# Decay broadcasts on SP's queue, and the first block's decays behind the latest eviction, in a hybrid SSD and linear-attention layer

## The chip, the cores and the metric

The kernel runs on one core of a Trainium2 chip. The metric is the device time of one execution in microseconds (us), lower is better. Engines are named as in the profile: PE (TensorE, matrix multiplies), PEld (its weight loads), DVE (VectorE), ACT (ScalarE), POOL (GpSimd), SP (SyncE, which here only issues DMAs). "ACTq" and "SPq" are rows in which ACT or SP issues a DMA. Every engine works through its own queue in order.

## The reference

One decoder layer on 2048 tokens, 1024 channels wide, with 16 learned tokens ahead, in float32. One wide projection of the normalised input feeds a Mamba-2 scan (SSD, 16 heads in 4 groups, chunks of 128), gated linear attention (GLA, 4 heads) and the merge gates.

```python
u = rmsnorm(hres, norm_w)
proj = jnp.einsum('bld,dn->bln', u, w_in)
z, xbc, dt_raw, q, k, v, g_gla, a_lr, merge_g = split_cols(proj, IN_WIDTHS)
xbc = jax.nn.silu(causal_depthwise_conv(xbc, conv_w, conv_b))
...
da_cum = jnp.cumsum(da, axis=-1)
seg = da_cum[..., :, None] - da_cum[..., None, :]
decay = jnp.exp(jnp.where(causal, seg, -jnp.inf))
scores = jnp.einsum('bzthn,bzshn->bhzts', cc, bc)
y_diag = jnp.einsum('bhzts,bzsh,bzshp->bzthp', scores * decay, dtc, xc)
...
o_r, _ = gla_chunked(q[:, m:], k[:, m:], v[:, m:], log_a[:, m:], GLA_CHUNK, st_m)
...
merged = jnp.sum(gates * branch_proj, axis=2)
return hres + jnp.einsum('bld,de->ble', merged, w_out)
```

The change is about `decay`, a 128 x 128 matrix for each head and chunk.

## The kernel before

The tokens are worked through in four blocks of 512 (blocks 0 to 3; block 0 also has the 16 learned tokens). In each block the projections run one after the other: for the SSD groups 0 to 3 a `z` projection and four feature projections, then the four GLA heads. Behind the four blocks come the merge gates, the branch products and the output product. Every float32 product is done as three products of split operands (L189, L190, L191).

A weight is loaded by SP as `wr` in block 0 (L179, three buffers), copied to its high part by ACT (L169), subtracted by POOL to its low part (L170), both in `whl` (four buffers), and stored to DRAM (L185) behind the two that follow it, so SP waits for POOL there. In blocks 1 to 3 SP loads the finished `whl` back (L165).

A projection accumulates in PSUM banks of `pj`, of which there are three. In block 0 a feature projection takes two banks of 264 columns, later one of 512. ACT evicts a bank by L491 and L492, DVE runs the convolution over it (three passes of L496), ACT makes a tanh (L499), and DVE finishes (L500). ACT's L454, with DVE's L453, evicts the banks of the GLA gates.

A scan of a group (`ssd_scan`) runs beside the projections of the next group, one step for each projection. `before(c)` prepares chunk c: PE transposes, and the decays. For these, `fetch_cb` broadcasts four rows of the cumulated sums from DRAM (`cumd`, stored once in a block at L429) to all 128 partitions as `cb`, 256 KB, in three buffers: the broadcast of a chunk waits until the Relus that read the buffer three chunks ago are done. ACT then makes four Relus (L569) and an Exp (L571) into `sq`, DVE multiplies by the masked scores (L572), and PE uses the product one step later in `after(c)` (L581). `before(c)` asks for the broadcast of chunk c + 1.

The order on PE and SP is that of the source, in `tc.manual_schedule`. On ACT, DVE and POOL a scheduler orders the instructions by estimated times, so an instruction can stand there far ahead of its place in the source. `tc.issue_after(ins)` binds the instructions of its block to stand behind `ins` in their engine's queue, without a semaphore. The broadcasts were issued from ACT's queue, where the scheduler placed them too.

Of the kernel before, what the change touches and what calls it, by code (L numbers as in the profile page):

```python
# [1 line left out]

# [9 lines left out]
AF = mybir.ActivationFunctionType  # L12
ALU = mybir.AluOpType

P = 128
# [3 lines left out]
BLK = 512  # L19
# [14 lines left out]
QSCALE = 128.0 ** -0.5  # L34
# [8 lines left out]
def trunk_kernel(ctx: ExitStack, tc: tile.TileContext, xm, xmt, w_feat, w_tok, w_zm, w_br, w_o,  # L43
                 cf32, cmsk, pvec, fnw, hvec, gw2, out):
    nc = tc.nc
# [288 lines left out]
    hcw = const.tile([P, 16, 4], F32, name="hcw")  # L334
    nc.vector.tensor_scalar(hcw, conv_w, 0.5, None, op0=ALU.mult)
    hcb = const.tile([P, 16], F32, name="hcb")
# [130 lines left out]
    def ssd_proj(o, g):  # L467
# [10 lines left out]
            yield from proj_tok(f"z{g}", w_tok[g], o.u, o.starts, places)  # L478
            done = [(ps, zs[:, 2 * r:2 * r + 2].rearrange("p c f -> p (c f)")) for r, ps in enumerate(pss)]
        for ps, dst in done:  # L480
            nc.scalar.activation(dst, ps, AF.Tanh, scale=0.5)
            nc.vector.scalar_tensor_tensor(dst, dst, 1.0, ps, op0=ALU.add, op1=ALU.mult)
        yield
        for j in range(4):
            ti = g * 4 + j
            pss = proj_feat(f"s{ti}", w_feat[T_SSD + ti], o.segs_all, o.mov)
            cin = mk(spool, [P, 3 + META + BLK], F32, "cin")
            acc = mk(spool, [P, META + BLK], F32, "acc")[:, :tt]
            nc.scalar.activation(cin[:, 0:3], tails[:, ti, :], AF.Copy)
            for ps, (a, n) in zip(pss, o.segs_all):  # L490
                nc.scalar.activation(cin[:, 3 + a:3 + a + n], ps[:, :n], AF.Copy)  # L491
                nc.scalar.activation(acc[:, a:a + n], ps[:, :n], AF.Identity, scale=hcw[:, ti, 3:4],  # L492
                                     bias=hcb[:, ti:ti + 1])
            nc.gpsimd.tensor_copy(tails[:, ti, :], cin[:, tt:tt + 3])
            for k in range(3):
                nc.vector.scalar_tensor_tensor(acc, cin[:, k:k + tt], hcw[:, ti, k:k + 1], acc,  # L496
                                               op0=ALU.mult, op1=ALU.add)
            f = mk(wk, [P, META + BLK], F32, "act", bufs=NACT)
            nc.scalar.activation(f[:, :tt], acc, AF.Tanh)  # L499
            nc.vector.scalar_tensor_tensor(f[:, :tt], f[:, :tt], 1.0, acc, op0=ALU.add, op1=ALU.mult)  # L500
            feats.append(f)
            yield
        begin(ssd_scan(o, g, feats, zs))

    cbs = {}

    def fetch_cb(o, g, c):
        cbs[g, c] = cb = mk(spool, [P, 4, P], F32, "cb", bufs=3)
        nc.scalar.dma_start(cb, o.cumd[4 * g:4 * g + 4, c * P:(c + 1) * P].unsqueeze(0).to_broadcast([P, 4, P]))

    def ssd_scan(o, g, feats, zs):
        m0, ci0 = o.m0, o.ci0
        tkd, tkc, wde, ecu, dec = o.tkd, o.tkc, o.wde, o.ecu, o.dec
# [8 lines left out]
        if m0:  # L522
            ps = bank(pt, "pt")
# [15 lines left out]
        for c in range(NCH):  # L539
            a = m0 + c * P  # L540
# [8 lines left out]
        def before(c):  # L549
            a = m0 + c * P  # L550
            ci = ci0 + c
            if c + 1 < NCH:
                fetch_cb(o, g, c + 1)
            cb = cbs.pop((g, c))
            ps = bank(pt, "pt")
# [9 lines left out]
            bt = mk(wk, [P, P], F32, "bt")  # L565
            nc.scalar.activation(bt, ps[:, 256:384], AF.Copy)
            dm = mk(wk, [P, 4, P], F32, "sq", bufs=NSQ)
            for h in range(4):
                nc.scalar.activation(dm[:, h], cb[:, h], AF.Relu, scale=-1.0,  # L569
                                     bias=tkc[:, ci, 4 * g + h:4 * g + h + 1])  # L570
            nc.scalar.activation(dm, dm, AF.Exp, scale=-1.0)  # L571
            nc.vector.tensor_tensor(dm, dm, scm[:, c].unsqueeze(1).to_broadcast([P, 4, P]), op=ALU.mult)  # L572
            held[c] = xdt, xw, bt, dm

# [38 lines left out]
        for j in range(2):  # L613
            ps = bank(pt, "pt")
# [7 lines left out]
    def gla_proj(o, h):  # L622
# [1 line left out]
        t0 = T_GLA + 4 * h  # L624
        qs = mk(wk, [P, META + BLK], F32, "act", bufs=NACT)
        ps, = proj_feat(f"g{t0}", w_feat[t0], o.segs_real, o.mov)
        nc.scalar.activation(qs[:, :BLK], ps, AF.Copy, scale=QSCALE)
        yield
        kf = mk(wk, [P, META + BLK], F32, "act", bufs=NACT)
        for ps, (a, n) in zip(proj_feat(f"g{t0 + 1}", w_feat[t0 + 1], o.segs_all, o.mov), o.segs_all):  # L630
            nc.scalar.activation(kf[:, a:a + n], ps[:, :n], AF.Copy)
        yield
        vh = mk(wk, [P, NCH, 256], F32R, "tok4", bufs=NT4)
        vl = mk(wk, [P, NCH, 256], F32R, "tok4", bufs=NT4)
# [737 lines left out]
```

## Time and profile before

| | |
|---|---|
| median of 3 runs | 2281.77 us (2281.37 to 2286.51) |
| the profiled execution's own time | 2279.31 us |
| its span, first to last instruction | 2277.5 us |
| busy: PE, PEld | 2227.8 us (98%), 1944.2 us (85%) |
| busy: DVE, ACT, POOL | 1548.0 (68%), 1182.4 (52%), 681.9 us (30%) |
| mean granted clock of PE | 0.995 |
| DMA queue of SP | 402.84 MB, 54.4% of 16 engines' span |
| DMA queue of ACT | 112.88 MB, 14.2% of 16 engines' span |
| `cb` broadcasts | 64 of 256 KB, median 5.6 us from issue to landing |

A row of the timeline gives start, duration, engine, line, operation, output tile `<-` input tiles, shapes and a count of merged instructions; in square brackets stands how long the engine had been idle and what ended that. The tables of waits give the engine and line that waited, the releaser, total us, times, and the longest. A busy PE is not a PE at its peak, since the ends of matmuls are modelled; the granted clock and the count of matmuls in a stretch say more.

### The profile page before, as it was taken

Reading aid. Unit: us, or ns where it says so; the run is one execution under the profiler, and the core shown is the slowest. Engines: PE = TensorE matmul, PEld = TensorE weight load, DVE = VectorE, ACT = ScalarE, POOL = GpSimd, SP = SyncE. Lnnn points to the kernel's source line nnn. Section 1 sums busy time; section 2 is a strip of 40 time slices with the busy share of each in tenths; the row PEclk is TensorE's granted clock in tenths of the full one; section 3 lists DMA queues with packets and bytes.
Section 4 is the critical chain, followed back from the end, with each engine's and each line's share of the span. In section 5 each row is a group of like instructions: output and inputs, shape, how many; then the busy total and the mean of one; then the engine's idle time right before and its main releaser. Section 6 shows DMA issues by size and latency. Waiting matters only on the chain.

```text
span 2277.5 us, 36482 instructions
## 1 busy us (share of the span) xinstructions
PE 2227.8 (98%) x12653; PEld 1944.2 (85%) x12653; DVE 1548.0 (68%) x2899; ACT 1182.4 (52%) x2731; POOL 681.9 (30%) x681
## 2 busy tenths in 40 slices
PE   7899999999999999999999999999999999999998
PEld 6899989888888988888988898878888888888887
DVE  5777676675667667567568665684688954689876
ACT  5665655465534455544456453454554545554544
POOL 4344433122221122212122200056323264323341
PEclk9999999999999999999999999999999999999999
DMA  9766776667787667778676654377677866687753
GB/s 312 231 204 218 273 259 209 219 203 230 251 266 228 217 219 220 250 245 269 194 226 220 216 196 158 111 224 230 206 258 261 308 223 202 227 289 265 247 188 126
DMA packets 301544, 518.04 MB, mean 227 GB/s; under 512 B 27696, under 2 KB 143664, under 8 KB 301360
## 3 DMA queue, kind: packets, MB, share of 16 engines
q1 hardware_dynamic: 200400, 402.84, 54.4%
q10 hardware_dynamic: 100960, 112.88, 14.2%
q8 instruction: 99, 1.62, 0.3%
q14 instruction: 85, 0.70, 0.1%
HBM read 368.42 MB, written 147.19 MB: 226 GB/s over the span
## 4 chain that ended last, share of the span: by engine, by line
PE 81%; DMA 5%; DVE 5%; ACT 4%; issue 3%; POOL 2%; SPq 0%; ACTq 0%; POOLq 0%; DVEq 0%
PE pj L189 19%; PE pj L191 18%; PE pj L190 18%; PE pt L189 3%; PE pt L190 3%; PE pt L191 3%; PE pc L581 2%; PE pc L189 2%; PE pc L191 2%; PE pc L190 2%; PE pc L732 2%; PE pc L582 1%; PE pc L584 1%; DMA acc<-in_xmt 1%; PE pc L840 1%
## 5 line engine op out<-in xcount | busy, mean ns | idle before, releaser
L189 PE MATMUL pj<-ue,whl 128*128 128x264 f32 (+1 forms) x672 | 238.7, 355 | 12.8 <-ACT acc L492 6.5
L191 PE MATMUL pj<-ue,whl 128*128 128x264 f32 (+1 forms) x672 | 232.0, 345 | 0.8 <-DVE tkc L399 0.8
L190 PE MATMUL pj<-ue,whl 128*128 128x264 f32 (+1 forms) x672 | 230.9, 344 | 0.0
L189 PE MATMUL pj<-uo,whl 128*128 128x512 f32 x512 | 206.6, 403 | 0.0
L191 PE MATMUL pj<-uo,whl 128*128 128x512 f32 x512 | 200.1, 391 | 0.0
L190 PE MATMUL pj<-uo,whl 128*128 128x512 f32 x512 | 199.4, 390 | 0.0
L82 POOL TENSOR_TENSOR wr<-wr 128x256 f32<-128x256 f32 x80 | 67.0, 837 | 434.8 <-DMA wr<-u 176.3
L189 PE MATMUL pj<-b,a 128*128 128x512 f32 (+1 forms) x484 | 188.9, 391 | 2.3 <-ACT sn L1018 1.7
L190 PE MATMUL pj<-b,a 128*128 128x512 f32 (+1 forms) x484 | 187.9, 388 | 1.0 <-DVE b L959 0.9
L191 PE MATMUL pj<-b,a 128*128 128x512 f32 (+1 forms) x484 | 188.8, 390 | 0.0
L170 POOL TENSOR_TENSOR whl<-wr,whl 128x512 fp32r<-128x512 f32 (+1 forms) x100 | 135.1, 1358 | 177.4 <-ACT whl L169 131.0
L496 DVE SCALAR_TENSOR_TENSOR acc<-cin,hcw,acc 128x512 f32<-128x512 f32 (+1 forms) x192 | 154.7, 806 | 27.0 <-ACT acc L492 26.0
L974 POOL TENSOR_TENSOR as<-ar,ar 128x512 f32<-128x512 f32 x40 | 57.0, 1424 | 382.8 <-DMA ar<-in_w_br 145.0
L984 DVE TENSOR_TENSOR a<-ar,a 128x512 fp32r<-128x512 f32 x160 | 127.5, 805 | 60.7 <-ACT a L983 58.4
L189 PEld LDWEIGHTS pj<-ue,whl 128*128 128x128 f32 x672 | 128.7, 192 | 30.4 <-ACT acc L492 7.5
L959 DVE TENSOR_TENSOR b<-br,b 128x512 fp32r<-128x512 f32 x140 | 122.1, 892 | 44.3 <-ACT b L958 43.9
L189 PE MATMUL pj<-whl,ue 128*128 128x256 f32 (+1 forms) x496 | 143.8, 290 | 1.5 <-ACT ue L315 1.5
L189 PE MATMUL pj<-whl,uo 128*128 128x256 f32 (+1 forms) x496 | 143.3, 289 | 0.5 <-DMA whl<-k_zm 0.5
L191 PEld LDWEIGHTS pj<-ue,whl 128*128 128x128 f32 x672 | 128.7, 192 | 16.0 <-POOL whl L170 1.0
L191 PE MATMUL pj<-whl,ue 128*128 128x256 f32 (+1 forms) x496 | 140.3, 283 | 1.7 <-DVE ue L317 1.7
L190 PEld LDWEIGHTS pj<-ue,whl 128*128 128x128 f32 x672 | 128.9, 192 | 14.7
L191 PE MATMUL pj<-whl,uo 128*128 128x256 f32 (+1 forms) x496 | 140.9, 284 | 0.0
(318 smaller groups left out, 6538.3 us busy)
## 6 DMA issues: line engine op xcount, KB each, us to landing
whl<-k_s SPq DMA_DIRECT2D x96, 512.0 KB, 4.4
whl<-k_g SPq DMA_DIRECT2D x96, 512.0 KB, 4.2
whl<-k_v SPq DMA_DIRECT2D x48, 512.0 KB, 3.7
whl<-k_z SPq DMA_DIRECT2D x36, 512.0 KB, 3.8
wr<-in_w_feat SPq DMA_DIRECT2D x64, 256.0 KB, 4.3
k_s<-whl SPq DMA_DIRECT2D x32, 512.0 KB, 3.6
cb<-cumd ACTq DMA_DIRECT2D x64, 256.0 KB, 5.6
y<-gg ACTq DMA_DIRECT2D x64, 256.0 KB, 4.5
```

Source lines behind the costliest of these rows:

```text
L82: nc.gpsimd.tensor_tensor(o, x, y, op=ALU.subtract)
L170: nc.gpsimd.tensor_tensor(hl[:, 1], raw, hl[:, 0].bitcast(F32), op=ALU.subtract)
L189: nc.tensor.matmul(ps, sh, mh, start=first, stop=False, **kw)
L190: nc.tensor.matmul(ps, sh, ml, start=False, stop=False, **kw)
L191: nc.tensor.matmul(ps, sl, mh, start=False, stop=last, **kw)
L496: nc.vector.scalar_tensor_tensor(acc, cin[:, k:k + tt], hcw[:, ti, k:k + 1], acc, op0=ALU.mult, op1=ALU.add)
L581: nc.tensor.matmul(py[:, h * 64:(h + 1) * 64], dm[:, h], xdt[:, h], start=True, stop=True)
L582: nc.tensor.matmul(py[:, 256:512], cf[:, a:a + P], s_ssd[:, g], start=True, stop=True)
L732: nc.tensor.matmul(ps[:, r * P:(r + 1) * P], kq[:, 2 * r * P:(2 * r + 1) * P], kq[:, (2 * r + 1) * P:(2 * r + 2) * P], start=True, stop=True)
L959: nc.vector.tensor_tensor(t[:, 1], raw, t[:, 0].bitcast(F32), op=ALU.subtract)
L974: nc.gpsimd.tensor_tensor(s1, a21, a22, op=ALU.add)
L984: latest[:] = [nc.vector.tensor_tensor(t[:, 1], src, t[:, 0].bitcast(F32), op=ALU.subtract)]
```

## The change

`fetch_cb` issues its DMA from SP, whose queue stands in source order, instead of ACT. A list `evicted` keeps the latest traced eviction of a projection by ACT, and in block 0 the Relus and the Exp of a chunk's decays are bound to stand behind it in ACT's queue. Nothing else is computed. The lines behind the edits move by one to five.

```diff
-from contextlib import ExitStack
+from contextlib import ExitStack, nullcontext
...
         for ps, dst in done:
-            nc.scalar.activation(dst, ps, AF.Tanh, scale=0.5)
+            evicted[:] = [nc.scalar.activation(dst, ps, AF.Tanh, scale=0.5)]
...
                 nc.scalar.activation(cin[:, 3 + a:3 + a + n], ps[:, :n], AF.Copy)
-                nc.scalar.activation(acc[:, a:a + n], ps[:, :n], AF.Identity, scale=hcw[:, ti, 3:4],
-                                     bias=hcb[:, ti:ti + 1])
+                evicted[:] = [nc.scalar.activation(acc[:, a:a + n], ps[:, :n], AF.Identity, scale=hcw[:, ti, 3:4],
+                                                   bias=hcb[:, ti:ti + 1])]
...
-    cbs = {}
+    cbs, evicted = {}, []
+
+    def behind():
+        return tc.issue_after(evicted[-1].ins) if evicted else nullcontext()
+
 
     def fetch_cb(o, g, c):
         cbs[g, c] = cb = mk(spool, [P, 4, P], F32, "cb", bufs=3)
-        nc.scalar.dma_start(cb, o.cumd[4 * g:4 * g + 4, c * P:(c + 1) * P].unsqueeze(0).to_broadcast([P, 4, P]))
+        nc.sync.dma_start(cb, o.cumd[4 * g:4 * g + 4, c * P:(c + 1) * P].unsqueeze(0).to_broadcast([P, 4, P]))
...
             dm = mk(wk, [P, 4, P], F32, "sq", bufs=NSQ)
-            for h in range(4):
-                nc.scalar.activation(dm[:, h], cb[:, h], AF.Relu, scale=-1.0,
-                                     bias=tkc[:, ci, 4 * g + h:4 * g + h + 1])
-            nc.scalar.activation(dm, dm, AF.Exp, scale=-1.0)
+            with behind() if o.b == 0 else nullcontext():
+                for h in range(4):
+                    nc.scalar.activation(dm[:, h], cb[:, h], AF.Relu, scale=-1.0,
+                                         bias=tkc[:, ci, 4 * g + h:4 * g + h + 1])
+                nc.scalar.activation(dm, dm, AF.Exp, scale=-1.0)
...
-        nc.scalar.activation(qs[:, :BLK], ps, AF.Copy, scale=QSCALE)
+        evicted[:] = [nc.scalar.activation(qs[:, :BLK], ps, AF.Copy, scale=QSCALE)]
...
-            nc.scalar.activation(kf[:, a:a + n], ps[:, :n], AF.Copy)
+            evicted[:] = [nc.scalar.activation(kf[:, a:a + n], ps[:, :n], AF.Copy)]
```

How ACT's queue changes at the start of the scan of group 1 in block 0 (the stretch around 136 us of the profile). `sq_240`, `sq_269`, `sq_288` and `sq_306` are the decays of chunks 0 to 3, `cb_...` their broadcasts, `pj_241` and `pj_242` the two banks of the projection that PE has just finished. Before:

```order
L530 ACTIVATE bt_230_1772<-pt_228_1766 16x128
L569 ACTIVATE sq_240_1796<-cb_222_1691,tkc_39_392 128x128 x4
L569 ACTIVATE sq_269_1991<-cb_235_1783,tkc_39_392 128x128 x4
L569 ACTIVATE sq_288_2106<-cb_264_1978,tkc_39_392 128x128 x4
L571 ACTIVATE sq_240_1796<-sq_240_1796 128x512
L509 DMA cb_283_2093<-cumd_43_396 128x4x128
L566 ACTIVATE bt_239_1794<-pt_236_1785 128x128
L169 ACTIVATE whl_276_2017<-wr_277_2019 128x512
L571 ACTIVATE sq_269_1991<-sq_269_1991 128x512
L509 DMA cb_322_2325<-cumd_43_396 128x4x128
L571 ACTIVATE sq_288_2106<-sq_288_2106 128x512
L509 DMA cb_335_2417<-cumd_43_396 128x4x128
```

Then come L569 for `sq_306` and the evictions of `pj_241` and `pj_242`. After:

```order
L534 ACTIVATE bt_230_1772<-pt_228_1766 16x128
L574 ACTIVATE sq_240_1796<-cb_222_1691,tkc_39_392 128x128 x4
L576 ACTIVATE sq_240_1796<-sq_240_1796 128x512
L570 ACTIVATE bt_239_1794<-pt_236_1785 128x128
L169 ACTIVATE whl_276_2017<-wr_277_2019 128x512
L491 ACTIVATE cin_247_1867<-pj_241_1803 128x264
L492 ACTIVATE acc_248_1868<-pj_241_1803,hcb_378,hcw_376 128x264
L491 ACTIVATE cin_247_1867<-pj_242_1804 128x264
L492 ACTIVATE acc_248_1868<-pj_242_1804,hcb_378,hcw_376 128x264
```

The Relus and Exps of chunks 1 to 3 have moved from ahead of these evictions to a place behind those of later projections, one chunk behind each; the broadcasts have left the queue.

Where a moved decay now stands, for chunk 1 of group 0 (`sq_164`), behind the evictions of `pj_150` and `pj_151` (around 100 us of the profile):

```order
L491 ACTIVATE cin_156_1293<-pj_151_1230 128x264
L492 ACTIVATE acc_157_1294<-pj_151_1230,hcb_378,hcw_376 128x264
L574 ACTIVATE sq_164_1320<-cb_129_1103,tkc_39_392 128x128 x4
L169 ACTIVATE whl_197_1517<-wr_198_1519 128x512
L570 ACTIVATE bt_163_1318<-pt_160_1309 128x128
L576 ACTIVATE sq_164_1320<-sq_164_1320 128x512
L499 ACTIVATE act_158_1304<-acc_157_1294 128x528
```

The rows L574 and L576 are new at this place; the rest stood there before in the same order.

And SP's queue in block 0, around 100 to 110 us, after (`cb_222` and `cb_235` are the broadcasts for chunks 0 and 1 of group 1):

```order
L179 DMA wr_217_1615<-in_w_tok 128x512
L513 DMA cb_222_1691<-cumd_43_396 128x4x128
L185 DMA k_s7_1_1523<-whl_197_1517 128x1024
L179 DMA wr_224_1695<-in_w_tok 128x512
L185 DMA k_z2_0_1612<-whl_214_1606 128x1024
L179 DMA wr_226_1702<-in_w_tok 128x512
L513 DMA cb_235_1783<-cumd_43_396 128x4x128
L185 DMA k_z2_1_1619<-whl_216_1613 128x1024
L179 DMA wr_244_1807<-in_w_feat 128x512
```

The two L513 rows are new between the loads and stores of weights, which keep their order.

## The prediction

> **What bounds the kernel now.** TensorE (PE) is busy nearly all of the span (the table above), so only time in which PE stands still, or runs at a lower granted clock, can be won back. I first asked who PE waited for in the first block, from 60 to 200 us (columns: total us, times, longest):
>
> ```profile
> PE pj L189 <- ACT acc L492: 6.1, 4, 4.2
> PE pj L189 <- ACT g_all L454: 4.4, 2, 3.1
> ```
>
> These two rows are all of it. Both releasers are ScalarE (ACT) instructions that empty a PSUM bank of `pj`, which has three. No wait is for a weight. The timeline of PE places them; in brackets stands the idle time before the row:
>
> ```profile
> 81.94 0.59 PE L189 MATMUL pj<-ue,whl 128*128 128x264 f32 x1 [3.10 <-ACT g_all L454]
> ...
> 90.66 0.39 PE L189 MATMUL pj<-ue,whl 128*128 128x264 f32 x1 [0.51 <-ACT acc L492]
> ...
> 99.71 0.39 PE L189 MATMUL pj<-ue,whl 128*128 128x264 f32 x1 [0.87 <-ACT acc L492]
> ...
> 110.03 0.39 PE L189 MATMUL pj<-ue,whl 128*128 128x264 f32 x1 [1.26 <-ACT g_all L454]
> ...
> 144.68 0.59 PE L189 MATMUL pj<-ue,whl 128*128 128x264 f32 x1 [4.21 <-ACT acc L492]
> ...
> 193.70 0.39 PE L189 MATMUL pj<-ue,whl 128*128 128x264 f32 x1 [0.55 <-ACT acc L492]
> ```
>
> The table by stretches adds the clock (behind the busy times of PE, PEld, DVE, ACT and POOL, with counts, stands the granted clock):
>
> ```profile
> 80.00:100.00 20.00, 16.68 (x115) 15.69 (x116) 13.21 (x24) 16.32 (x39) 4.50 (x4) 0.91 0.57 184
> 100.00:120.00 20.00, 18.74 (x147) 17.90 (x147) 17.38 (x37) 14.00 (x33) 8.21 (x11) 1.00 0.59 198
> 120.00:140.00 20.00, 20.00 (x163) 19.34 (x163) 13.67 (x30) 12.67 (x38) 9.56 (x7) 1.00 0.48 162
> 140.00:160.00 20.00, 15.79 (x108) 15.47 (x109) 14.19 (x21) 11.99 (x31) 7.47 (x8) 0.83 0.79 268
> ```
>
> Behind the gap of 3.10 us the mean clock is 0.91, behind that of 4.21 us it is 0.83: (1 - 0.91) x 20 = 1.8 us and (1 - 0.83) x 20 = 3.4 us of full clock not granted. So each long gap is paid twice.
>
> What does ACT do while PE waits? At the first gap:
>
> ```profile
> 77.25 1.55 ACT L569 ACTIVATE sq<-cb,tkc 128x128 f32<-128x128 f32 x5
> ...
> 78.71 1.26 ACT L569 ACTIVATE sq<-cb,tkc 128x128 f32<-128x128 f32 x4
> ...
> 80.75 0.61 ACT L571 ACTIVATE sq<-sq 128x512 f32<-128x512 f32 x1
> ...
> 81.43 0.46 ACT L454 ACTIVATE g_all<-pj,pv 128x264 f32<-128x264 f32 x1
> ...
> 84.17 1.28 ACT L569 ACTIVATE sq<-cb,tkc 128x128 f32<-128x128 f32 x4 [0.16 <-DMA cb<-cumd]
> ```
>
> And at the second, in the next group:
>
> ```profile
> 136.02 1.56 ACT L569 ACTIVATE sq<-cb,tkc 128x128 f32<-128x128 f32 x5
> ...
> 137.48 1.26 ACT L569 ACTIVATE sq<-cb,tkc 128x128 f32<-128x128 f32 x4
> ...
> 139.53 0.61 ACT L571 ACTIVATE sq<-sq 128x512 f32<-128x512 f32 x1
> ...
> 140.72 1.13 ACT L571 ACTIVATE sq<-sq 128x512 f32<-128x512 f32 x2
> 142.62 1.28 ACT L569 ACTIVATE sq<-cb,tkc 128x128 f32<-128x128 f32 x4 [0.77 <-DMA cb<-cumd]
> 143.80 0.37 ACT L491 ACTIVATE cin<-pj 128x264 f32<-128x264 f32 x1
> ```
>
> The Relus of three chunks stand in one block, ahead of the eviction that PE needs, though PE needs only chunk 0's decay soon. Chunks 1 to 3 are the avoidable part.
>
> **The change part by part.**
>
> *Decays moved, first gap.* Of the 12 Relus between 77.25 and 80.75 (3.50 us, 0.29 each) the changed order keeps four ahead of L454: 8 x 0.29 = 2.3 us go. The Exp of chunk 0 stays. L454 then starts near 79.1 instead of 81.43, PE resumes near 79.7 instead of 81.94, and some 0.9 us of the gap are left: 2.2 us won. If that short gap no longer drops the clock, 1.8 us more. The 0.51 us before 90.66 go too, because what is taken off ACT between 77 and 90 (8 Relus, the four of 84.17, three Exps of 0.61) is 2.3 + 1.3 + 1.8 = 5.4 us, more than PE comes earlier. Sum A: 2.2 + 1.8 + 0.5 = **4.5 us**.
>
> *Second gap.* Ahead of L491 now stand four Relus, one Exp and short pieces. What goes: 8 Relus (2.3), two Exps (1.1), the Relus of chunk 3 with the wait for their DMA (1.28 + 0.77). From 143.80 that is 5.5 us back, to 138.3, which is before PE stops at 144.68 - 4.21 = 140.47. So the gap goes altogether, and its clock: 4.21 + 3.4 = 7.6 us. By the counts it is less: 163 matmuls fill 20 us between 120 and 140 (0.123 us each), and 108 from 140 to 160, so 55 x 0.123 = 6.8 us were lost. I take the middle, **7.2 us**, and **0.5 us** for the same pattern at 193.70.
>
> [...]
>
> *Where the decays go.* Chunks 1 to 3 of the first three groups now stand behind the last eviction of a projection, 4 x 0.29 + 0.61 = 1.8 us each, 9 x 1.8 = 16 us in all, and they must fit ACT's idle time. The nearest rows are from group 0:
>
> ```profile
> 104.68 0.65 ACT L499 ACTIVATE act<-acc 128x528 f32<-128x528 f32 x1 [3.46 <-DVE acc L496]
> ...
> 109.50 0.48 ACT L454 ACTIVATE g_all<-pj,pv 128x264 f32<-128x264 f32 x1 [1.01 <-DVE tok L453]
> ...
> 103.82 0.76 DVE L496 SCALAR_TENSOR_TENSOR acc<-cin,hcw,acc 128x528 f32<-128x528 f32 x1
> ...
> 105.61 0.67 PE L581 MATMUL pc<-c,sq 128*128 128x64 f32 x5
> ...
> 81.40 0.69 DVE L572 TENSOR_TENSOR sq<-sq,sq 128x512 f32<-128x512 f32 x1 [0.79 <-ACT sq L571]
> ```
>
> Behind the evictions ACT waits 3.46 us for VectorE's (DVE's) convolution: chunk 1 fits there for nothing. Chunk 2 stands ahead of L454, where ACT idles only 1.01 us: 1.8 - 1.0 = 0.8 us are added to the gap at 110.03. DVE multiplies chunk 1's decay behind its convolution, which ends at 103.82 + 0.76 = 104.58; with 0.69 us for the multiply (the last row) it is ready near 105.3, and PE reads it at 105.61. With that margin of 0.3 us I charge another 0.4 us. Bounds: 0 (ACT's idle time takes all) to 1.8 us per chunk. Sum B: **-1.2 us**. A later decay also frees its `cb` buffer later, so SP waits longer; that comes next.
>
> *The DMAs moved to SP.* All 64 leave ACT's queue, and SP now holds everything behind a broadcast until its `cb` buffer is free and `cumd` is written. What stands behind it are weight loads.
>
> ```profile
> 54.92 0.38 SPq L179 DMA_DIRECT2D wr<-in_w_tok  x1
> ...
> 55.67 0.20 ACT L489 ACTIVATE cin<-tails 128x3 f32<-128x3 f32 x1 [0.37 <-DMA cumd<-cin]
> ...
> 61.10 0.63 ACT L169 ACTIVATE whl<-wr 128x512 fp32r<-128x512 f32 x1 [1.65 <-PE pj L191]
> ...
> 110.26 0.43 SPq L179 DMA_DIRECT2D wr<-in_w_feat  x1
> ...
> 124.77 1.14 ACT L169 ACTIVATE whl<-wr 128x512 fp32r<-128x512 f32 x2
> ...
> wr<-in_w_tok SPq DMA_DIRECT2D x28, 256.0 KB, 4.3
> cb<-cumd ACTq DMA_DIRECT2D x64, 256.0 KB, 5.6
> ```
>
> The first broadcast waits until about 55.7 for `cumd`; the load of 54.92 then leaves near 56.5 and lands 4.3 us later, at 60.8, just before the copy at 61.10. A later one waits for chunk 2's Relus, to about 112, so the load of 110.26 leaves 2 us late; its copy is at 124.77, 14.5 us behind the issue, of which 4.3 are transfer. Even a whole broadcast (5.6 us) ahead of it is covered. Without that cover each would cost its 1.6 to 2 us. I take 0.
>
> In blocks 1 to 3 the decays keep their clumps and the broadcast of chunk 3 waits for chunk 0's Relus. The worst place:
>
> ```profile
> 957.01 1.85 SPq L78 DMA_DIRECT2D wr<-y  x4
> ...
> 963.73 1.03 SPq L165 DMA_DIRECT2D whl<-k_g  x2
> ...
> 961.54 0.38 ACTq L509 DMA_DIRECT2D cb<-cumd  x1
> ...
> 964.58 0.53 ACTq L85 DMA_DIRECT2D br_t<-wr  x1
> ...
> 972.27 0.58 ACT L237 ACTIVATE tok<-pj 128x512 fp32r<-128x512 f32 x1
> ```
>
> The buffer is free at 961.54, when the old issue went out; SP reaches that point at 957.0. The four loads of L78 slip by 4.9 us, the weight load from 963.73 to about 964.4, and ACT's store L85, which waits in ACT's queue for POOL's work on those loads, from 964.58 to about 969.5, still ahead of the eviction at 972.27. That is tight at three such places (one in each block): bounds 0 and 3 x 2 us. I take **-0.6 us**. That ACT no longer issues 64 DMAs gains nothing there, since PE waits for none of them.
>
> Sum: 4.5 + 7.2 + 0.5 - 1.2 - 0.6 = **10.4 us**. The profiled execution took 2279.31 us, 1.81 beside its span of 2277.5, so it becomes 2268.9; the median of the runs shown, 2281.77, lies 2.5 us higher, and from it I forecast **2271.4 us**. After the first block PE runs nearly without gaps, so what is won there reaches the end.
>
> **The rivals.** About 0.3% (6.8 us) is what a measurement of this kernel can tell from no change.
>
> 1. *Group 0 gives its part back.* ACT and DVE are busy 14.00 and 17.38 of 20 us between 100 and 120, and two to three decays (3.6 to 5.4 us of ACT, 1.4 to 2.1 of DVE) are added. If DVE is the limit there, PE comes earlier only to wait longer: A is lost and B doubles, 7.7 - 2.4 - 0.6 = 4.7 us won, **2277.1**. For it: the thin margin before 105.61. Against it: the Exp and Ln chain of the gates, which feeds DVE, starts earlier as well. The group 1 term does not depend on this.
> 2. *It does not do what it says.* If the freed eviction meets another late instruction of ACT in the same place, the gaps stay: **2281.8**. Against it: nothing else stands there in the new order.
> 3. *Slower: PE waits for the late decays.* A decay now starts only when an eviction ends, and DVE's convolution is queued ahead of its multiply. The point where it decides is the 0.3 us margin: if DVE runs one convolution pass set late (from 100.8 to 104.6, 3.8 us), each of nine chunks (three in each of groups 0 to 2) makes PE wait some 3.5 us: 31 - 11 = 20 us lost, **2302**. Against it: chunk 2's and chunk 3's margins are wider than chunk 1's, since the gates' work lies between in the one and is over in the other.
>
> **How the numbers follow.** Forecast 0.63 (2267 to 2275), rival 1 0.19, rival 2 0.08, rival 3 0.10. If all six gaps went (10.5 us) with both clock losses (5.2), 15.7 us would be won: 2266.1. The range is 2265 to 2278: from a little under that bound to just above rival 1. Faster: the 0.63 and 0.07 of rival 1's better half, 0.70; same: 0.12 of rival 1 and rival 2, 0.20; slower: 0.10.
>
> **What would show it.** Right: at the starts of groups 1 and 2 PE has no gap over 0.5 us, the stretch from 130 to 150 has full clock, at group 0 a gap of about 1 us is left, and four Relus stand ahead of each eviction in place of twelve. Sum B: the gap by L454 near 105 grows by less than 1 us. Wrong: PE rows released by DVE's `sq` in block 0 (rival 3), a longer DVE-bound stretch between 85 and 115 (rival 1), or PE waits released by POOL's or a DMA's `whl` (a starved SP queue).

## The result and the profile after

| | before | after |
|---|---|---|
| median of 12 runs each, same chip | 2282.11 us (2281.07 to 2286.51) | 2276.40 us (2272.14 to 2280.35) |
| ratio after to before | | 0.9972, 95% interval 0.9963 to 0.9981 |
| profiled execution, span | 2279.31, 2277.5 us | 2279.3, 2277.5 us |

The change is 5.7 us faster by the medians (0.25%); the ratio, which is not the quotient of the medians, gives 0.28% (6.4 us). Its interval leaves no doubt of the sign, so the prediction's border of 0.3% for what can be measured was too wide. The two profiled executions took the same time. The one of before is among the fastest of its kernel, the one of after among the slowest of its own, so their ends cannot be subtracted. But PE runs the same 12653 matmuls in the same order in both, so the start of the k-th matmul can be compared between them. This offset (after minus before) is used below, mostly counted from 77 us, ahead of the first changed instruction at PE. What lies before is start-up: +0.9 us here, 0.0 to +3.3 us in the other runs. In the three kernels whose names begin with "gates" some matmuls near 77 us, in gates_first also near 106 us, stand in another order; counted from 70 us their offsets are 0.3 us closer to zero.

The table of PE's waits of after, from 60 to 200 us (total us, times, longest):

```profile
PE pj L189 <- ACT g_all L454: 2.6, 2, 1.5
PE pj L189 <- ACT acc L492: 1.4, 1, 1.4
PE pc L586 <- DVE sq L577: 0.5, 1, 0.5
```

PE's timeline of after has these rows at the same places:

```profile
80.93 0.39 PE L189 MATMUL pj<-ue,whl 128*128 128x264 f32 x1 [1.14 <-ACT g_all L454]
...
89.22 0.42 PE L189 MATMUL pj<-ue,whl 128*128 128x264 f32 x1 [1.39 <-ACT acc L492]
...
109.23 0.39 PE L189 MATMUL pj<-ue,whl 128*128 128x264 f32 x1 [1.49 <-ACT g_all L454]
...
124.75 0.44 PE L586 MATMUL pc<-c,sq 128*128 128x64 f32 x2 [0.45 <-DVE sq L577]
```

And the stretches of after (busy PE, PEld, DVE, ACT, POOL, then the granted clock):

```profile
80.00:100.00 20.00, 17.68 (x124) 16.90 (x125) 14.98 (x30) 15.26 (x36) 5.65 (x7) 0.91 0.62 202
100.00:120.00 20.00, 18.51 (x133) 17.66 (x132) 15.73 (x33) 15.53 (x38) 6.66 (x8) 0.91 0.58 185
120.00:140.00 20.00, 19.55 (x162) 19.19 (x161) 15.82 (x31) 12.71 (x36) 9.38 (x8) 1.00 0.53 162
140.00:160.00 20.00, 20.00 (x158) 19.30 (x157) 15.46 (x27) 13.84 (x36) 9.48 (x11) 1.00 0.83 301
```

The wait of 4.2 us at 144 and its half clock are gone: 158 matmuls from 140 to 160 instead of 108. The gap of 3.10 us at 82 has shrunk to 1.14 us, without half clock. But the gap of 0.51 us behind it has grown to 1.39, that by L454 from 1.26 to 1.49, and half clock stands behind both: 0.91 remains the mean in the first stretch and is new in the second.

ScalarE's timeline of after shows the two gaps as the change meant them. At the first:

```profile
78.20 1.26 ACT L574 ACTIVATE sq<-cb,tkc 128x128 f32<-128x128 f32 x4
79.50 0.63 ACT L576 ACTIVATE sq<-sq 128x512 f32<-128x512 f32 x1
80.05 0.28 ACT L570 ACTIVATE bt<-pt 128x128 f32<-128x128 f32 x1
80.39 0.48 ACT L454 ACTIVATE g_all<-pj,pv 128x264 f32<-128x264 f32 x1
```

At the second:

```profile
136.97 1.26 ACT L574 ACTIVATE sq<-cb,tkc 128x128 f32<-128x128 f32 x4
138.26 0.63 ACT L576 ACTIVATE sq<-sq 128x512 f32<-128x512 f32 x1
...
139.52 0.39 ACT L491 ACTIVATE cin<-pj 128x264 f32<-128x264 f32 x1
```

Four Relus stand ahead of each eviction. What made the gap at 89.22 stands between them, in ScalarE's timeline of after:

```profile
85.50 0.61 ACT L169 ACTIVATE whl<-wr 128x512 fp32r<-128x512 f32 x1
88.23 0.20 ACT L690 ACTIVATE gl<-g_all 128x1 f32<-128x1 f32 x1 [2.12 <-DVE g_all L462]
88.34 0.37 ACT L491 ACTIVATE cin<-pj 128x264 f32<-128x264 f32 x1
88.61 0.56 ACT L492 ACTIVATE acc<-pj,hcb,hcw 128x264 f32<-128x264 f32 x1
```

The scheduler put L690, a copy of one column for the GLA scan, ahead of the evictions; ACT stands still 2.12 us there for VectorE's scan of the gates, while the banks that PE wants are full. Before, that copy (L685) stood behind them, at 91.98.

In block 1 something new appears. PE's row, then ScalarE's, of after:

```profile
607.04 0.55 PE L586 MATMUL pc<-c,sq 128*128 128x64 f32 x3 [2.09 <-DVE sq L577]
```

```profile
598.34 0.64 ACT L281 ACTIVATE acc<-acc 128x512 f32<-128x512 f32 x1 [2.25 <-DMA acc<-in_xm]
...
600.59 0.41 ACT L574 ACTIVATE sq<-cb,tkc 128x128 f32<-128x128 f32 x1
600.74 1.62 ACTq L624 DMA_DIRECT2D y<-gg  x1
602.41 3.33 ACT L574 ACTIVATE sq<-cb,tkc 128x128 f32<-128x128 f32 x11 [1.41 <-issue]
605.64 0.61 ACT L576 ACTIVATE sq<-sq 128x512 f32<-128x512 f32 x1
```

Here the clump of 12 Relus (one at 600.59, eleven from 602.41) is whole, PE waits for chunk 0's decay behind it, and half clock follows (0.50 from 608.27 to 611.68 us): 3.9 us by the offset from 555 to 640 us. The clump came late twice over: ACT stood still 2.25 us for an input tile, and 1.41 us between the first Relu and the others, while it issued a DMA of L624.

The offset from 77 us, in us, for the change and the kernels of the next section, at PE's place in the program (times of before):

| kernel | 106 | 133 | 153 | 228 | 555 | 640 | 2270 |
|---|---|---|---|---|---|---|---|
| after | -2.0 | +0.5 | -6.2 | -7.1 | -7.4 | -3.5 | -1.0 |
| change_again | -2.0 | +0.5 | -6.3 | -7.1 | -6.7 | -3.3 | +3.9 |
| behind_only | -2.0 | +0.5 | -6.2 | -7.1 | -5.8 | -5.4 | -0.5 |
| sp_block0 | -2.0 | +0.5 | -6.3 | -7.2 | -6.8 | -6.8 | -4.4 |
| g0_free | 0.0 | 0.0 | -6.8 | -7.6 | -7.7 | -3.8 | -0.5 |
| sp_only | +0.1 | +0.1 | -0.9 | -1.2 | -1.1 | +1.0 | +4.1 |
| sp_late | -0.2 | -0.3 | -1.2 | -1.2 | -1.3 | +3.7 | +4.7 |
| gl_behind | -0.8 | +3.4 | -3.4 | -4.2 | -4.0 | -4.0 | -2.9 |
| behind_all | -3.5 | -0.2 | -6.9 | -7.8 | -4.6 | -2.6 | +2.7 |
| gates_first | -2.3 | -2.6 | -9.3 | -10.2 | -10.0 | -9.0 | -3.5 |
| gates_split | -5.6 | -1.6 | -8.4 | -9.2 | -9.1 | -8.9 | -6.9 |
| gates_split_sp0 | -5.7 | -0.5 | -7.3 | -8.1 | -7.9 | -6.7 | -7.4 |

Group 0 ends near 133. The change has won there 2.0 us by 106 and lost it by 133; the second gap is worth 6.7 to 6.8 us in every kernel in which the decays of group 1 are bound. Part of that belongs to the trace of before: there half clock stands for two windows of 3.41 us behind the gap (142.88 to 149.71), in sp_only and sp_late, where the gap is as long (4.22 and 4.14 us), for one, and there these two lose 1.0 us less than before.

What is won in block 0 is not all in the trace at the end (2270 us, the last matmuls): from 640 us on, after loses another 2.6 us, and behind_only, without SP's queue, loses 4.9 us. Some of it is the comparison: the trace of before is 2.8 us below the median of its kernel.

### The profile page after: what moved, and what is told of

It reads as the page before. It is cut to its first block, busy times and chain, and to the rows that moved or that the text cites. A ratio compares the mean times of both kernels' runs of the same rounds, so it can differ in the third digit from the quotient of the medians.

```text
span 2277.5 us, 36524 instructions
## 1 busy us (share of the span) xinstructions
PE 2229.0 (98%) x12653; PEld 1945.3 (85%) x12653; DVE 1552.6 (68%) x2899; ACT 1183.7 (52%) x2731; POOL 679.1 (30%) x681
## 4 chain that ended last, share of the span: by engine, by line
PE 77%; DMA 8%; DVE 6%; ACT 4%; issue 2%; POOL 1%; SPq 1%; ACTq 0%; POOLq 0%; DVEq 0%
PE pj L189 18%; PE pj L191 18%; PE pj L190 18%; PE pt L189 3%; PE pt L190 3%; PE pt L191 3%; PE pc L586 2%; PE pc L189 2%; PE pc L191 2%; PE pc L190 2%; DMA acc<-in_xmt 2%; PE pc L737 2%; PE pc L587 1%; PE pc L589 1%; DMA br<-out_t 1%
## 5 line engine op out<-in xcount | busy, mean ns | idle before, releaser
L189 PEld LDWEIGHTS pj<-ue,whl 128*128 128x128 f32 x672 | 128.5, 191 | 23.6 <-ACT g_all L454 3.1
L189 PE MATMUL pj<-whl,uo 128*128 128x256 f32 (+1 forms) x496 | 144.1, 291 | 0.3 <-DMA whl<-k_zm 0.3
L191 PEld LDWEIGHTS pj<-ue,whl 128*128 128x128 f32 x672 | 128.7, 192 | 16.0 <-POOL whl L170 1.0
L191 PE MATMUL pj<-whl,uo 128*128 128x256 f32 (+1 forms) x496 | 141.4, 285 | 0.0
L190 PE MATMUL pj<-whl,uo 128*128 128x256 f32 (+1 forms) x496 | 141.4, 285 | 0.0
```

The lines of the kernel that those rows point to most:

```text
L189: nc.tensor.matmul(ps, sh, mh, start=first, stop=False, **kw)
L190: nc.tensor.matmul(ps, sh, ml, start=False, stop=False, **kw)
L191: nc.tensor.matmul(ps, sl, mh, start=False, stop=last, **kw)
```

## The experiments

Each kernel was timed against the kernel before on the same chip. The ratios are the recorded ones; they differ from the quotients of the medians beside them by up to 0.15%:

| kernel | median us (runs) | before, same job | ratio, 95% interval |
|---|---|---|---|
| behind_only | 2279.34 (9) | 2282.41 | 0.9972, 0.9959 to 0.9984 |
| sp_only | 2288.41 (11) | 2282.41 | 1.0019, 1.0009 to 1.0028 |
| sp_block0 | 2277.02 (5) | 2282.41 | 0.9965, 0.9953 to 0.9978 |
| gl_behind | 2279.50 (10) | 2282.41 | 0.9980, 0.9969 to 0.9991 |
| behind_all | 2284.74 (11) | 2282.95 | 1.0010, 1.0000 to 1.0021 |
| g0_free | 2277.59 (12) | 2282.95 | 0.9977, 0.9968 to 0.9987 |
| gates_first | 2277.30 (11) | 2282.95 | 0.9973, 0.9965 to 0.9982 |
| gates_split | 2276.47 (12) | 2281.99 | 0.9976, 0.9967 to 0.9984 |
| gates_split_sp0 | 2274.03 (5) | 2281.99 | 0.9967, 0.9954 to 0.9979 |
| change_again | 2275.94 (12) | 2281.99 | 0.9972, 0.9962 to 0.9983 |
| sp_late | 2283.99 (12) | 2283.58 | 1.0008, 0.9996 to 1.0020 |

### The two halves of the change: behind_only, sp_only, sp_block0

behind_only has the bound decays and leaves the broadcasts on ACT's queue.

```diff
-        nc.sync.dma_start(cb, o.cumd...)
+        nc.scalar.dma_start(cb, o.cumd...)
```

> The decays of block 0 bound behind the evictions, all broadcasts still on ACT's queue. Theory (the binding alone makes the gain; SP's queue adds nothing and costs something in blocks 1 to 3): 2275 to 2277 us, gain of 5 to 7 us, all of it in block 0, the gaps of the first matmul behind group 1's start gone; no 2 us gap in the third group of block 1. Rival (the gain comes from taking the waits for the broadcast off ACT): 2281 to 2283 us.

The ratio is that of the change. The median, 3.1 us below before, lies between the two expected ranges. The offsets up to 228 us are those of the change to 0.1 us, with gaps of 1.14, 1.38 and 1.51 us and half clock behind the last two. So the gain in block 0 comes from the binding alone.

sp_only is the other half: broadcasts on SP's queue, no decay bound.

```diff
-            with behind() if o.b == 0 else nullcontext():
+            with nullcontext():
```

> All broadcasts on SP's queue, the decays not bound. Theory: the clump of twelve Relus stays ahead of the evictions, so the gaps of about 3 and 4 us with their half clock stay: 2281 to 2284 us. Rival (ACT's waits for the broadcast were the cost): 2275 to 2278 us.

Slower than before, by 0.19% (0.09 to 0.28), and above both expected ranges. The gaps of 3.11 and 4.22 us stay with their half clocks. The broadcasts' queue alone wins nothing.

sp_block0 is the change with the broadcasts of blocks 1 to 3 back on ACT's queue.

```diff
-        nc.sync.dma_start(cb, o.cumd...)
+        (nc.sync if o.b == 0 else nc.scalar).dma_start(cb, o.cumd...)
```

> As the change, but the broadcasts of blocks 1 to 3 go back to ACT's queue. Theory that SP's queue in blocks 1 to 3 costs (the gap of 2.09 us near 605 us and the half clock behind it, 3.9 us in the profiled execution): 2270 to 2273 us and no such gap. Rival (that gap is chance, or comes from elsewhere): as the change, 2275 to 2278 us.

The loss of 3.9 us between 555 and 640 us is absent (0.0), as the theory had it; but the median, 2277.02, lies where the rival had it, and the ratio, 0.9965, cannot be told from the change's.

### Group 0: g0_free, gl_behind, gates_first, gates_split

g0_free leaves group 0 unbound.

```diff
-            with behind() if o.b == 0 else nullcontext():
+            with behind() if o.b == 0 and g > 0 else nullcontext():
```

> The change with group 0 of block 0 left unbound, so that only groups 1 to 3 of block 0 have their decays behind the evictions; all broadcasts on SP's queue as in the change. Theory (group 0 gives its part back, the second gap is the whole gain): the gap of 3.1 us and its half clock at 82 stay, those of 1.39 and 1.49 us with their half clocks do not come, the gap of 4.2 us at 140 stays away; the offset at 160 us is -6 to -7 as in the change and the time within 0.1% of it, 2274 to 2278. Rival (the prediction's own sum: group 0 wins A - B = 3.3 us): 2279 to 2281. Second rival: the 3.1 us gap stays and the later ones come too, because the order of group 1 reaches back: over 2281.

Its waits of PE from 60 to 200 us are those of before in group 0, without the second gap:

```profile
PE pj L189 <- ACT g_all L454: 4.5, 2, 3.3
PE pj L189 <- ACT acc L492: 0.9, 1, 0.9
```

The offset is 0.0 at 133 and -7.6 at 228, and the time that of the change within the intervals. Binding group 0 is worth nothing that these measurements could tell; the gaps at the starts of groups 1 and 2 (6.8 and 0.8 us) are the whole gain.

gl_behind binds the copies L688 and L690 behind the latest eviction too, so that the wait of 2.12 us at 88.23 cannot stand ahead of it.

```diff
-        nc.scalar.activation(gl[:, :NCH], grc[:, :, P - 1], AF.Copy, scale=ITEMP)
+        with behind() if m0 else nullcontext():
+            nc.scalar.activation(gl[:, :NCH], grc[:, :, P - 1], AF.Copy, scale=ITEMP)
         if m0:
-            nc.scalar.activation(gl[:, NCH:], gf[:, META - 1:META], AF.Copy, scale=ITEMP)
+            with behind():
+                nc.scalar.activation(gl[:, NCH:], gf[:, META - 1:META], AF.Copy, scale=ITEMP)
```

> As the change, and in block 0 the two small copies of the GLA scan (gl, L688 and L690), which the scheduler had put ahead of the evictions of group 0, bound behind the latest eviction too. Theory (the L690 that waits 2.1 us for DVE's scan makes the gap of 1.39 us at 87.8 us and the half clock behind it): both go, 2272 to 2274 us, gain on the change of 2 to 4 us. Rival (DVE is the limit between 85 and 115 us anyway): the gap moves to the next eviction, 2275 to 2278 us.

The gap of 1.39 us at 89 goes. But a larger one comes one projection later; PE's timeline of gl_behind:

```profile
98.43 0.39 PE L189 MATMUL pj<-ue,whl 128*128 128x264 f32 x1 [2.61 <-ACT acc L492]
```

With a wait of 1.9 us for `sq` near 126 and half clock behind both, 3.4 us are lost by 133. Moving one late instruction out of the way only moved the wait, as the rival had it.

gates_first takes the gates of block 0 ahead of the scan in each step of the source, and lets L454 count as an eviction, so chunks 0 and 2 of group 0 stand behind all four L454.

```diff
-                    nc.scalar.activation(g_all[:, h, a:a + n], ps[:, :n], AF.Abs, bias=gb)
+                    evicted[:] = [nc.scalar.activation(g_all[:, h, a:a + n], ps[:, :n], AF.Abs, bias=gb)]
...
-                begin(gates(o))
+                if b:
+                    begin(gates(o))
+                else:
+                    running.insert(0, gates(o))
```

> The change with the gates of block 0 taken ahead of the scan in the source's order of each step, and their eviction (L454 of the change) counted as an eviction, so that the decays of group 0's chunks 0 and 2 stand behind all four of them; the copies of gl fall behind the projection's evictions of themselves. Theory (in group 0 it is ScalarE's order around L454 that leaves the gaps of 1.14, 1.39 and 1.49 us, the last two with half clock): all three become gaps under 0.8 us, no half clock between 75 and 130 us, offset at 160 us near -14, time 2268 to 2272. Rival (VectorE is the limit between 85 and 115, as the copies of gl bound behind the evictions showed): L454 goes but gaps of 1.5 us or more come elsewhere between 85 and 130, released by VectorE's work or by an eviction that waits for it; time 2275 to 2279. Second rival: chunk 0's and chunk 2's decays are now too late for PE: rows of PE released by the masked decay, time over 2280.

From 77 to 96 us no gap is over 0.8 us, and 5.3 us are won against before (counted from 70 us). Then one comes inside the gates' own matmuls (lines move by two); PE's timeline of gates_first:

```profile
106.16 0.38 PE L453 MATMUL pj<-act,w 48*128 48x264 f32 x1 [2.65 <-ACT acc L494]
```

2.9 us go back there with its half clock (a mean of 0.91 from 100 to 120 us). The offset that the theory named, near -14 at 160 us, did not come (-9.3), and the time is the first rival's. At 228 us gates_first is 3 us ahead of the change, yet its median is not below the change's.

gates_split keeps that order for the first pair of heads alone and the order of the change for the second.

```diff
+                    if h2 == 0:
+                        evicted[:] = [ev]
...
+                if h == 1 and o.b == 0:
+                    running.append(running.pop(0))
```

> As gates_first, but the gates go ahead of the scan only for their first pair of heads; for the second pair the order of the change stays, with chunk 2's decays ahead of L454. Theory (group 0's first part can be won by the order around the first L454, what is lost at the second pair is a separate price): as with the gates first, no gap over 0.8 us between 75 and 95 us and 5 us won there; at the second pair a gap of about 1.5 us as in the change, with half clock if the grid cuts it so (1.7 us); offset at 160 us near -10, time 2271 to 2275. Rival (what is won early in group 0 is always given back by 115 us, whatever the order, since VectorE and ScalarE have a fixed amount of work to get through by then): offset at 160 us again -6 to -7, time 2275 to 2279.

Again 5.6 us are won by 106, and 4.0 lost by 133: most of it at two waits from 103 to 107, the longest for the gates' eviction (now L456), with half clock behind, and 0.7 us at one for `sq`. The offset at 160 us, -8.4, lies between theory and rival. The table of waits of gates_split from 60 to 200 us:

```profile
PE pj L189 <- ACT g_all L456: 2.1, 1, 2.1
PE pj L189 <- ACT acc L498: 1.1, 2, 0.9
PE pj L453 <- ACT acc L498: 0.6, 1, 0.6
PE pc L592 <- DVE sq L583: 0.5, 1, 0.5
```

So what is won early in group 0 is mostly given back by 133 us: in four orders it nets +3.4 (gl_behind), +0.5 (the change), -1.6 (gates_split) and -2.6 us (gates_first). gates_split_sp0, with the order of gates_split in block 0, nets -0.5, with two windows of half clock in group 0 instead of one, so by an estimate from these two runs about 1 us between two orders can be the clock alone. A fixed amount of work would make them equal, which they are not by more than that, but none of these orders keeps the 5 us. Between 80 and 120 us of after, DVE is busy 30.7 and ACT 30.8 of 40 us; whether their waits for each other set the limit was not isolated.

### Blocks 1 to 3: behind_all, sp_late, gates_split_sp0

behind_all binds the decays in all blocks.

```diff
-            with behind() if o.b == 0 else nullcontext():
+            with behind():
```

> The change with the decays of blocks 1 to 3 bound behind the evictions as well. Theory (in blocks 1 to 3 it is the clump of Relus ahead of the first Exp that, with a late broadcast on SP's queue, makes PE wait): the wait of 2.09 us for VectorE's masked decay near 605 us and the half clock behind it go, and the offset against the kernel before stays near -6 us past block 1; time 2271 to 2275. Rival (PE's later losses are noise of the queues and the clock, the clump has no part in it): gaps of the same size appear at other places, time 2275 to 2279, not to be told from the change. Second rival: the bound decays come too late in the later blocks, where PE has more matmuls per projection but the scan's own steps are as dense: PE rows released by the masked decay in blocks 1 to 3, time over 2282.

The wait near 605 goes, and others come. Its waits of PE from 420 to 1420 us:

```profile
PE pc L586 <- DVE sq L577: 5.6, 10, 1.3
```

Ten waits for late decays, and 0.10% slower than before (0.00 to 0.21), where the change is 0.28% faster: the second rival's account and time. In blocks 1 to 3 the clump is the better order, so block 0 alone is to be bound.

sp_late is the kernel before with the broadcasts of blocks 1 to 3 on SP's queue.

```diff
-        nc.scalar.dma_start(cb, o.cumd...)
+        (nc.sync if o.b else nc.scalar).dma_start(cb, o.cumd...)
```

> The kernel before, with no decay bound and the broadcasts of blocks 1 to 3 alone on SP's queue; block 0 is as before. Theory (SP's queue costs in blocks 1 to 3, where the broadcast of chunk 3 holds loads behind it): slower than before by 1 to 6 us, 2283 to 2288, with a PE wait of 1.5 us or more near 613 us released by the masked decay. Rival (the loss seen with all broadcasts on SP and no decay bound, 0.19%, comes from block 0 and the start): within 1 us of before, no PE wait over 1 us between 580 and 640 us.

PE's timeline of sp_late has the wait again:

```profile
613.34 0.32 PE L586 MATMUL pc<-c,sq 128*128 128x64 f32 x1 [2.31 <-DVE sq L577]
```

With its half clock it loses 5.0 us between 555 and 640, the sign that the theory named. The times do not confirm it: the median is 0.4 us above before, and the ratio's interval reaches from -0.9 to +4.6 us.

gates_split_sp0 is gates_split with ACT's queue for the broadcasts of blocks 1 to 3, as in sp_block0.

> The kernel with the gates' first pair ahead of the scan, with the broadcasts on SP's queue in block 0 alone and on ScalarE's in blocks 1 to 3. Theory (SP's queue costs something in block 1, where a wait of about 2 us near 605 us was seen with all broadcasts on SP and none with them on ScalarE): no gap over 1.5 us between 580 and 640 us, and 1 to 4 us faster than the same kernel with all broadcasts on SP. Rival (no part in the time): the two within 1 us of each other.

It has the lowest median of all, 2274.03 us (5 runs), 8 us below before and 2.4 us below gates_split, as the theory had it. But the intervals of this kernel, of gates_split and of the change overlap, so a version that surely beats the change was not found. Nor does the theory's cause fit: gates_split, with all broadcasts on SP, has no such wait near 605 either.

Over all traces: a wait of 1.6 to 2.3 us between 605 and 615 stands in five of the eight that have SP's queue in blocks 1 to 3 and the clump (after, change_again, g0_free, sp_only, sp_late). In the other three, where group 0's order differs, gl_behind and gates_split have none over 0.45 us and gates_first one of 0.59. Of the four with ACT's queue there, three have none (before among them), and gates_split_sp0 has one of 0.97 us, released by DVE's `sq` too. So SP's queue goes with the long wait, but is neither enough for it nor needed for a short one. In after and sp_late ACT stood still 2.25 and 2.99 us ahead of the clump for a tile of the next block's input (L281), whose load SP issues behind a broadcast; in behind_only it was 1.93 us, without a wait of PE. That this load is the cause is likely but was not isolated; in after the issue of L624 added 1.41 us, in sp_late 0.15.

### The price of a gap: change_again and clock_probe

change_again is the change once more, for a second trace.

> The change itself once more, for a second trace of the same program. Theory (the clock's grid decides what a gap costs beyond its length): the same gaps of 1.1, 1.4 and 1.5 us in group 0, but half clock not necessarily behind the same ones; a window of 3.413 us that holds more than about 0.45 of idleness is followed by half clock, one that holds less than 0.4 is not; time 2274 to 2279. Rival (the clock follows the gap itself): half clock again behind the gaps of 1.4 and 1.5 us and the one of 2 us near 605 us, and behind no other.

The same gaps of 1.14, 1.38 and 1.49 us to 0.01 us in group 0, the same half clocks behind the last two (0.50 from 89.02 to 92.43 us behind the first of them), and again behind the one near 605, here only 1.57 us long. That they came back alike separates nothing. One place does: near 1480 us both traces have a gap of 1.92 or 1.93 us, and only change_again has half clock there. First a window of after with the next, then one of change_again with the next (tables of stretches):

```profile
1478.67:1482.08 3.41, 1.87 (x13) 1.18 (x11) 3.41 (x7) 0.75 (x2) 0.00 (x0) 1.00 0.84 246
1482.08:1485.49 3.41, 1.98 (x12) 1.54 (x12) 2.31 (x4) 1.73 (x4) 0.00 (x0) 1.00 0.96 326
```

```profile
1478.25:1481.66 3.41, 1.63 (x12) 0.93 (x9) 3.41 (x7) 0.60 (x1) 0.00 (x0) 1.00 0.99 251
1481.66:1485.07 3.41, 2.94 (x12) 2.79 (x13) 2.69 (x6) 2.18 (x5) 0.00 (x0) 0.50 1.00 351
```

In the window of change_again PE is idle for 1.78 us in all, in that of after for 1.54, and only in change_again does half clock follow. So the same gap of one program cost clock in one execution and not in the other.

clock_probe measures the clock alone.

```diff
+    for n in range(160):
+        links, width = SHAPES[n % len(SHAPES)]
+        burst = 130 + (state >> 8) % 32
+        for k in range(burst):
+            nc.tensor.matmul(ps[:, :264], wt, x[:, :264], start=k == 0, stop=k == burst - 1)
+        prev = ps
+        for _ in range(links - 1):
+            nc.scalar.activation(t[:, :width], prev[:, :width], AF.Copy, scale=0.001)
```

> A kernel of its own, which computes nothing of the reference: 160 bursts of 130 to 161 matmuls of 128x264, after each of which PE waits for a chain of one to eight ScalarE copies, so that gaps of eight lengths from about 1 to 4 us fall at changing places of the clock's grid. Theory (the clock is set anew every 3.413 us, and is halved for the next such window when PE stood still for more than about 0.45 of the last one, 1.5 us): gaps under 1.3 us are never followed by half clock; from 1.5 to 3 us some are and some are not, by how the grid cuts them, in about 0.55 (1.5 us) rising to all (3 us); and sorting by the idle share of the window tells them apart with few exceptions. Rival (the length of the gap alone decides): one length from which all are followed by half clock, below which none is. Second rival (a whole window of idleness is needed): none below 3.4 us.

Each length of gap came some 20 times; the number that half clock followed:

| gap, us | 0.93 | 1.39 | 1.84 | 2.30 | 2.75 | 3.21 | 3.66 |
|---|---|---|---|---|---|---|---|
| gaps | 20 | 20 | 20 | 20 | 20 | 20 | 19 |
| half clock behind | 0 | 0 | 10 | 11 | 13 | 15 | 19 |

The eighth length came out under 0.5 us and is left out. Every stretch of half clock in the probe is one or two windows of 3.413 us long, on a grid of 3.413 us. Two windows of the probe's table of stretches, each with the next (columns as above):

```profile
226.06:229.47 3.41, 2.02 (x16) 1.81 (x16) 0.00 (x0) 1.24 (x3) 0.00 (x0) 1.00 0.03 7
229.47:232.89 3.42, 3.42 (x31) 3.42 (x30) 0.00 (x0) 0.00 (x0) 0.00 (x0) 1.00 0.00 0
406.97:410.38 3.41, 1.57 (x13) 1.36 (x12) 0.00 (x0) 1.66 (x4) 0.00 (x0) 1.00 0.00 0
410.38:413.79 3.41, 3.41 (x17) 3.41 (x18) 0.00 (x0) 0.00 (x0) 0.00 (x0) 0.50 0.00 0
```

In the first, PE was idle for 1.39 us, and full clock stands in the next; in the second for 1.84 us, and half clock stands in the next, with 17 matmuls instead of 31. Sorted so, 3 of the probe's 882 windows at full clock stand on the wrong side of a bound of 0.54 idle. The expected bound of 0.45 was too low for the probe; both rivals, a length that decides and a whole idle window, fall. Of the 80 gaps of 1.84 to 3.21 us, 31 had no half clock behind them: even at 3.21 us 5 of 20, where the theory had none.

## Why the prediction came out as it did

The forecast was 2271.4 us, range 2265 to 2278, faster; 2276.4 us were measured, inside the range, with the right sign. 5.7 us (6.4 by the ratio) were won where 10.4 were forecast. The time lies inside because the range reached to rival 1: the second gap came out as reckoned, the gain in group 0 not at all. By its steps, in the offsets of after (each from 1 to 2 us before the gap to where PE runs evenly again):

| step | predicted | measured |
|---|---|---|
| first gap and its clock (2.2 + 1.8) | 4.0 won | 3.3 won |
| the 0.51 us before 90.66 | 0.5 won | 2.4 lost |
| decays behind the evictions, sum B | 1.2 lost | 1.4 lost |
| second gap | 7.2 won | 6.8 won |
| 193.70 | 0.5 won | 0.8 won |
| SP's queue, blocks 1 to 3 | 0.6 lost | 3.9 lost in block 1 of the trace; from block 0's end on 0.7 to 1.4 for all causes together, if its 7.1 won are held against 6.4 (ratio) or 5.7 (medians) |

**The second gap** was right in cause and size. The count of matmuls had given 6.8; the clock term was too large because it charged all 6.83 us of half clock, of which PE stood still for 1.80. With half the work done at half clock (17 matmuls in a window of the probe instead of 31), (6.83 - 1.80) / 2 = 2.5, and with 4.21 that is 6.7. About 1 us of it is luck, by an estimate from sp_only and sp_late: there one window of half clock stands behind the gap, and they lose 1.0 us less. The same holds for the first gap: 1.96 us shorter, and (3.41 - 0.50) / 2 = 1.5 of clock, 3.4 against the measured 3.3. The step that was mis-sized is "(1 - clock) x 20".

**Sum A failed at its last term**: "The 0.51 us before 90.66 go too, because what is taken off ACT between 77 and 90 ... is 5.4 us". The load was taken off, but the scheduler filled the freed place: L690 came ahead of the evictions and ACT stood there 2.12 us for DVE. In the order of ACT's queue it could have been read: the copy had moved past the four instructions that evict the two banks. gl_behind shows that this copy made that wait, and also that without it the wait returns elsewhere.

**Sum B** came out as a sum of other parts than foreseen: the gap by L454 grew by 0.23 us, less than the 0.8 charged, but got half clock (1.78 lost in all); PE waited 0.45 us for `sq` at 124.75 (0.73 lost), the sign that was named for rival 3; and the 0.87 us before 99.71 went, which the sum had left out (1.14 won).

Together group 0 lost 0.5 us where 3.3 were to be won. **Rival 1**, "group 0 gives its part back", thus named the outcome: 2277.1 us. Its reason, DVE as the limit, is not shown: orders with the same work differ by 6 us at 133 us.

**SP's queue in block 0** at nothing: right, the offsets with and without it agree to 0.1 us at 228. **In blocks 1 to 3** the place was wrong: not loads of weights or the store L85 near 965, but the clump of Relus behind a late input tile near 605. How much of it stays in the median is open: the profiles say 2 to 5 us, behind_only, without it, loses 6.5 us from 228 us to the end and after 6.1, the medians of sp_block0 and of the change agree within their intervals, and sp_only (slower by 0.19%) and behind_only against the change (no difference) disagree on what SP's queue costs.

**Rival 2**, that the gaps stay, fell with the second gap. But what it describes, another late instruction of ACT in the freed place, is what L690 was at 89.22, and "nothing else stands there in the new order" was wrong for that eviction. **Rival 3** did not occur in block 0, apart from 0.45 us; behind_all brought it about in blocks 1 to 3.

## What to carry to other kernels

When a block of work is moved off a queue that a scheduler orders, read the new order at every later wait that the estimate removes: another instruction can take the freed place, and one that waits for another engine can cost more than was won there (here 2.4 us against 0.5). Price a PE gap by what the trace at hand shows behind it: here its length plus half of PE's busy time at half clock (4.21 + 2.5 = 6.7 us for the second gap, against 6.8 measured). Half clock stood here behind a window with 1.84 us of 3.41 idle in the probe, 1.78 near 1480 us and 1.39 in group 0, and none behind one with 1.54 near 1480 us. A gain inside one stretch of tightly coupled engines should be carried on to the end of that stretch before it is counted; here 2 to 5.6 us were won by 106 us and mostly gone by 133.

## What the runs showed of the hardware that was not expected

In the probe's trace all changes of PE's clock lie on a grid of 3.413 us, and a bound of 1.84 us of idleness in a window parts those with half clock behind them from the others but for 3 of 882. In the traces of before and after, from 40 us on, eight full-clock windows of that grid have half clock behind them, with 1.39, 1.49, 1.78 and, in five, 2.1 to 3.3 us idle; of the others the idlest have 1.54, 1.43 and 1.29 us. None of the eight was idle as a whole.

In group 0 of the kernel less idleness had half clock behind it than in the probe: behind the gap of 1.39 us it stood, behind none of the probe's 20 gaps of that length. First one window of after with the next, then one of before with the next, where 1.26 us idle had full clock behind them (tables of stretches):

```profile
86.03:89.44 3.41, 2.02 (x12) 1.34 (x11) 3.41 (x9) 1.29 (x6) 1.28 (x1) 1.00 0.36 136
89.44:92.85 3.41, 3.41 (x17) 3.41 (x17) 3.37 (x8) 2.97 (x9) 1.59 (x2) 0.50 0.42 121
```

```profile
108.75:112.16 3.41, 2.15 (x18) 2.13 (x18) 3.41 (x8) 1.36 (x3) 1.10 (x1) 1.00 0.97 306
112.16:115.57 3.41, 3.41 (x30) 3.41 (x29) 2.13 (x5) 3.21 (x8) 1.05 (x1) 1.00 0.27 86
```

PE is as busy in 86.03 to 89.44 as in the probe's 226.06 to 229.47 (2.02 us), but not with the same work. PE's timeline of after has in that window and in the one ahead of 109.92:

```profile
86.58 0.69 PE L538 MATMUL pc<-c,bt 16*128 16x256 f32 x2
...
106.65 0.28 PE L451 MATMUL pt<-act,w 48*128 48x264 f32 x1
```

By their shapes these multiply over 16 and 48 partitions, the others over 128. The equal busy times hold different counts, too, and the ends of matmuls are modelled: 12 matmuls make up the 2.02 us in after, 16 in the probe. Why 1.39 us idle had half clock behind it in after and not in the probe is not shown: no run changed the shapes, or the count of matmuls, alone.
